# A hybrid decoder layer on one core: another order of the kept weights in memory

## The chip, the cores and the metric

The kernel runs on one core of a Trainium2 chip. The metric is the device time of one execution in microseconds (us), taken as the median of several runs. A core has five engines with a queue of instructions each: TensorE (PE, matrix products; its weight loads are listed as PEld), VectorE (DVE), ScalarE (ACT), GpSimd (POOL) and SyncE (SP), which here only issues transfers. Sixteen DMA engines carry the transfers of the core.

## The reference

One layer over 2048 rows of width 1024, all in float32. A conditioning vector gives shift, scale and gate; the input is normalised, scaled and shifted, and one projection of width 2832 feeds four heads of gated linear attention and eight query heads of attention in a sliding window:

```python
mod = jnp.dot(jax.nn.silu(c), w_ada[l]) + b_ada[l]
shift, scale, gate = jnp.split(mod, 3, axis=-1)
h = rmsnorm(x, g_norm[l]) * (1.0 + scale[:, None, :]) + shift[:, None, :]
proj = jnp.einsum('bsd,de->bse', h, w_in[l])
gq, gk, gv, ga, gz, sq, sk, sv, sz = split_cols(proj, COL_SIZES)
...
y = jnp.einsum('bse,ed->bsd', jnp.concatenate([o_gla, o_swa], axis=-1), w_out[l])
x = x + gate[:, None, :] * y
return rmsnorm(x, g_final)
```

The change concerns only how the parts of `w_in` are kept between their uses.

## The kernel before

**Split weights.** Each float32 weight is split into a high part (rounded to the matrix engine's float32r type) and a low part (the rest). A product is three matmuls: high by high, high by low, low by high. The input weights are therefore read once from the input `in_w_in`, split by ACT (a cast) and POOL or DVE (a subtraction), used, and both parts are stored in a tensor in memory called `wc`, from which later row blocks load them.

**Slots and row blocks.** The 2048 rows go in four blocks of 512 (`u` = 0 to 3). The 2832 columns are nine slots: six "half" slots of 256 columns (qk0, gz0, sz0, qk1, gz1, sz1; two pieces `c` of 128 columns, eight k tiles of 128 rows each) and three wide ones (kv with 272 columns, sq and gv with 512; four pieces `j` of two k tiles). Block 0 starts with qk0, gz0 and sz0 together, with k as the outer loop (`proj_t_outer`, line 943): each k step loads 384 KB of raw weights (`wr_first`), splits them (`part`, line 682) and prepares the normalised input of that k (`hh`, `hl`). After that come sz1/0, gz1/0, kv and so on, one slot after the other; the matmuls of these are called pt (half slots) and pn (wide ones).

**Where the first three slots live.** `first_w` (line 665) puts qk0 into two tiles of 8 KB a partition, `wh_first` and `wl_first`, for the high and the low part; each holds k, column. gz0 and sz0 lie in 16 small tiles of 2 KB a partition, `wh_own` and `wl_own` for each k, each with slot and column. The two first tiles come from the ring of five large weight tiles (`w_tile`, line 414), which the streamed slots use as well: pieces of kv take over the buffers of wh_first, wl_first and then of the sz1/0 tile, and can be filled only when the stores out of these have been done.

**The stores.** `keep_k` (line 693) stores an own tile; two of them (k = 0) go early, those of the last two k after the input's last tile (`keep_parts`, line 701), then the four stores of the first tiles, and the other ten own stores later, behind slot kv (`keep_rest`, line 711).

**Streamed slots.** `slot_w` (line 734) loads the pieces of the other slots. For block 0 it brings raw pieces, splits them into the tile and stores the whole tile; for later blocks it loads the tile from `wc` in two transfers of half the k tiles each (lines 766 and 767).

**What sets the order.** The kernel's own planner (class `Order`) takes each instruction with an estimated duration and writes a fixed order for every engine before anything runs. A DMA counts there by its bytes, an ACT or POOL instruction by a fixed part and its columns. All transfers of the weights go through SP's single queue in that order. A buffer is reused when everything that read it is done.

**Places in memory.** `wc` has one row of 2 × 22656 numbers per partition. A slot's part is ordered piece, part (high or low), k, column.

Of the kernel before, what the change touches and what calls it, by code (L numbers as in the profile page):

```python
# [9 lines left out]
F32 = mybir.dt.float32  # L10
F32R = mybir.dt.float32r
I32 = mybir.dt.int32
AF = mybir.ActivationFunctionType
ALU = mybir.AluOpType
# [4 lines left out]
P = 128  # L19
D = 1024  # L20
S = 2048
KT = D // P
NB = 512
# [19 lines left out]
SLOT_O = {}  # L43
# [7 lines left out]
HB, ZS, VB, GB, QR, WAB, STB, WB = 13, 6, 6, 4, 4, 5, 3, 5  # L51
# [288 lines left out]
def free_size(ap):  # L340
    n = 1
    for d in list(ap.shape)[1:]:
        n *= d
    return n
# [48 lines left out]
def layer_kernel(ctx, tc, x, xT, w_ada, w_gate, b_cols, b_gate, g_cols, c_cols, pos, inv_freq,  # L393
# [3 lines left out]
    V, A, G, SY = [Engine(od, e) for e in ("V", "A", "G", "SP")]  # L397
# [12 lines left out]
    hp = Pool("hp", HB)  # L410
# [3 lines left out]
    def w_tile(name):  # L414
        own = next(w_turn) % WB == WB - 1
        return wp.tile([P, 2 * KT * P], F32R, name=name, tag="w2" if own else "w", bufs=1 if own else WB - 1)
# [7 lines left out]
    def f(ap):  # L424
        return ap.bitcast(F32)


    def mmul(o, l, r, start, stop, bank=None):
        n, m, k = free_size(r), free_size(l), l.shape[0]
        mode = cell = None  # L430
        if l.dtype == F32:
            dur = 2 * max(0.107, n / 1200)
            if k <= 64:
                mode, cell = "rows", l.start_partition()
            elif m <= 64:
                mode, cell = "cols", o.start_partition()
        else:
            dur = max(0.112, n / 2400 + 0.0137)
        return od.add("PE", lambda: T.matmul(o, l, r, start=start, stop=stop), dur,  # L439
                      [l, r] + ([] if start else [o]), [bank if start and bank is not None else o],  # L440
                      mode=mode, cell=cell)
# [82 lines left out]
    near = Pool("near", 1)  # L524
    begin = Pool("begin2", 1, into=ctx2)
# [135 lines left out]
    wc = dram.tile([P, 2 * W_COLS], F32R, name="wc")  # L661
# [3 lines left out]
    def first_w():  # L665


        n = SLOT_N["qk0"]
        t0 = [w_tile(f"w{i}_first").rearrange("p (k n) -> p k n", n=n) for i in "hl"]
        t1 = [[hp.tile([P, 2, n], F32R, name=f"w{'hl'[i]}_own{k}", tag="hh" if i == 0 else "hl")  # L670
               if k < KT - 2 else
               near.tile([P, 2, n], F32R, name=f"w{'hl'[i]}_own{k}", tag=f"qk{i}" if k == KT - 2 else "zs",
                         bufs=2 if k == KT - 2 else ZS)
               for k in range(KT)] for i in range(2)]
        src = w_in[:, 0:3 * KT * n].rearrange("p (k n) -> p k n", n=3 * n)
        raws = {}

        def load(k):
            raws[k] = begin.tile([P, 3, n], F32, name=f"wr_first{k}", tag="st0", bufs=3)
            SY.dma_start(raws[k].rearrange("p a b -> p (a b)"), src[:, k])  # L680

        def part(k):
            raw = raws.pop(k)
            both = ([t[:, k] for t in t0], raw[:, 0]), ([t[k] for t in t1], raw[:, 1:3])
            for d, r in both:
                (G.tensor_copy if k == 0 else A.copy)(d[0], r)
            for d, r in both:
                G.tensor_tensor(d[1], r, f(d[0]), ALU.subtract)
            if k == 0:
                for i in range(2):  # L690
                    keep_k(i, 0)

        def keep_k(i, k, lift=None):
            o = 2 * SLOT_O["gz0"]
            to = wc[:, o:o + 4 * KT * n].rearrange("p (s c i k m) -> p s c i k m", s=2, c=2, i=2, k=KT)
            od.lift = LATER if lift is None else lift
            x = SY.dma_start(f(to[:, :, :, i, k]), f(t1[i][k]).rearrange("p s (c m) -> p s c m", c=2))
            od.lift = 0
            return x

        def keep_parts(after):
            ops = [keep_k(i, k, 0) for k in (KT - 1, KT - 2) for i in range(2)]
            o = 2 * SLOT_O["qk0"]
            to = wc[:, o:o + 2 * KT * n].rearrange("p (c i k m) -> p c i k m", c=2, i=2, k=KT)
            for i in range(2):
                for c in range(2):
                    ops.append(SY.dma_start(f(to[:, c, i]), f(t0[i][:, :, c * P:(c + 1) * P])))
            for x in ops:
                x.deps.add(after)

        def keep_rest():
            after = od.ops[-1]
            for i in range(2):
                for k in range(1, KT - 2):
                    keep_k(i, k, 0).deps.add(after)

        parts = [[[t0[i][:, k] for k in range(KT)] for i in range(2)]]
        for j in range(2):
            parts.append([[t1[i][k][:, j] for k in range(KT)] for i in range(2)])
        return parts, load, part, keep_parts, keep_rest  # L720

    stream, loaded = [], [2, 0]
# [11 lines left out]
    def slot_w(u, name, lift=LIFT):  # L734

        name, _, half = name.partition("/")
        n = SLOT_N[name]
        o = SLOT_O[name]
        wide = name in WIDE
        count = KT // 2 if wide else 2  # L740
        kk, m = (2, n) if wide else (KT, P)
        tiles = {}
        kept = wc[:, 2 * o:2 * (o + KT * n)].rearrange("p (j i k m) -> p j i k m", j=count, i=2, k=kk)
        src = w_in[:, o:o + KT * n].rearrange("p (j k m) -> p j k m", j=count, k=kk)
        step = max(1, NB // m)

        def load(j):
            t = w_tile(f"w_{name}{u}_{j}")[:, :2 * kk * m].rearrange("p (i k m) -> p i k m", i=2, k=kk)
            tiles[j] = t
            od.lift = -lift  # L750
            if u == 0:
                for k in range(0, kk, step):
                    turn = next(raw_turn)
                    if turn < 4 or turn % 7 < 3:
                        raw = stp.tile([P, NB], F32, name=f"wr_{name}{u}_{j}{k}", tag="st")
                    else:
                        raw = keep.tile([P, NB], F32, name=f"wr_{name}{u}_{j}{k}", tag="wst", bufs=4)
                    raw = raw[:, :step * m].rearrange("p (k m) -> p k m", k=step)
                    h_, l_ = [t[:, i, k:k + step] for i in range(2)]
                    SY.dma_start(raw, src[:, j, k:k + step])  # L760
                    A.copy(h_, raw)
                    (G if name in SPLIT_G else V).tensor_tensor(l_, raw, f(h_), ALU.subtract)
                od.lift = STORE
                SY.dma_start(f(kept[:, j]), f(t))
            else:
                for k in range(0, kk, kk // 2):
                    SY.dma_start(f(t[:, :, k:k + kk // 2]), f(kept[:, j, :, k:k + kk // 2]))

        stream.extend([lambda j=j: load(j) for j in ([int(half)] if half else range(count))])

        def w(i, k, c=0):
            return tiles[k // 2][:, i, k % 2] if wide else tiles[c][:, i, k]

        return w

# [7 lines left out]
    hh = [None] * KT  # L783
    hl = [None] * KT
# [58 lines left out]
    def halves(j):  # L843

        return [slice(0, NB // 2), slice(NB // 2, NB)] if j == 0 else [slice(0, NB)]
# [97 lines left out]
    def proj_t_outer(ws, each):  # L943

        ps = []
        for tag in ("mm", "mm", "psc", "psc", "px", "pqk"):
            b = 2 if tag in ("mm", "psc") else 1
            ps.append((mm if tag == "mm" else att).tile([P, NB], F32, name=f"po{len(ps)}", tag=tag, bufs=b))
        for k in range(KT):
            each(k)  # L950
            for h in halves(k):
                for i, w in enumerate(ws):
                    for ct in range(2):
                        cs = slice(ct * P, (ct + 1) * P)
                        p = ps[2 * i + ct]

                        for n, (a, b) in enumerate(((w[0], hh), (w[1], hh), (w[0], hl))):
                            mmul(p[:, h], a[k][:, cs], b[k][:, h], k == 0 and h.start == 0 and n == 0,
                                 k == KT - 1 and n == 2, p)
        return ps  # L960

# [13 lines left out]
    qk = {}  # L975
# [430 lines left out]
    sin = const.tile([P, 16, 32], F32, name="sin")  # L1406
    todo = [(0, n) for n in ORDER0] + [(u, n) for u in range(1, NU) for n in ORDER]
    ws = [slot_w(u, n, LIFT if i > 1 else 0) for i, (u, n) in enumerate(todo)]

    warm(WARM0, None)  # L1410
# [59 lines left out]
    for i, (u, slot) in enumerate(todo):  # L1470
        if u > 0 and slot == ORDER[0]:
            hh, hl = nexth[u]
        w = ws[i]
        name, _, half = slot.partition("/")
# [103 lines left out]
```

## Time and profile before

| what | value |
|---|---|
| median of three runs | 836.94 us (835.5, 836.94, 837.18) |
| the profiled execution | 835.71 us |
| its span, first to last instruction | 834.0 us |
| mean granted TensorE clock | 0.997 of full |
| HBM read, written | 145.26 MB, 54.66 MB |

The page of the profile has the busy time of each engine over the whole span. Other views used below: busy time by stretches, each engine's timeline (start, duration, engine, line, operation, output<-inputs, shape, count, and in brackets the idle time before it with what ended it), the instructions of one tile with their shortest, median and longest duration, and the table of DMA issues (destination<-source, count, size of one, median time to landing). Nearly every instruction is recorded by a helper, so its line is 387 or 439, and instructions are told apart by the names of their tiles.

### The profile page before, as it was taken

What the parts mean: (1) busy time and instruction counts of PE and PEld (TensorE: products, weight loads), DVE (VectorE), ACT (ScalarE), POOL (GpSimd) and SP (SyncE); (2) the same over time, 40 slices, a digit from 0 to 9 for tenths busy, and PEclk for the clock granted to TensorE, in tenths of its full rate; (3) what the DMA queues carried; (4) which work ended last, traced back from release to release, by engine and by line L of the source; (5) the groups of instructions that cost most, each with busy time, mean ns of one, the idle gap of its engine ahead of it and who ended that gap; (6) DMA issues with size and microseconds to landing.
All of it is one profiled execution on the core that took longest, in us unless ns stands there. A gap on an engine that the chain in (4) does not pass through costs nothing.

```text
span 834.0 us, 13255 instructions
## 1 busy us (share of the span) xinstructions
PE 809.6 (97%) x4274; PEld 671.9 (81%) x4274; DVE 597.4 (72%) x1140; ACT 511.0 (61%) x1271; POOL 396.0 (47%) x461
## 2 busy tenths in 40 slices
PE   7998999999999999999999999999999999999995
PEld 6777788879888787888878888888888888888884
DVE  6986567678568978785797747524675766889895
ACT  4567865898556778675587857524677633344431
POOL 4512225456632558645667544322462514665642
PEclk9999999999999999999999999999999999999998
DMA  9969997847448499598887938637467864454432
GB/s 339 377 196 354 388 357 297 288 150 267 174 169 286 142 370 332 180 327 307 284 296 271 380 117 301 219 111 267 143 209 265 288 216 166 141 162 152 140 101 101
DMA packets 118812, 200.81 MB, mean 241 GB/s; under 512 B 10275, under 2 KB 42070, under 8 KB 116054
## 3 DMA queue, kind: packets, MB, share of 16 engines
q1 hardware_dynamic: 117734, 199.91, 68.8%
q8 instruction: 34, 0.56, 0.3%
q14 instruction: 36, 0.29, 0.1%
q10 hardware_dynamic: 1008, 0.05, 0.1%
HBM read 145.26 MB, written 54.66 MB: 240 GB/s over the span
## 4 chain that ended last, share of the span: by engine, by line
PE 67%; DVE 3%; ACT 2%; DMA 2%; POOL 2%; issue 1%; DVEq 0%; ACTq 0%; POOLq 0%
PE pt L439 18%; PE pn L439 17%; PE ya L439 10%; PE ys L439 9%; PE ppo L439 3%; PE psc L439 2%; PE po L439 2%; DMA xt<-in_xT 1%; PE ppt L444 1%; PE pc L439 1%; DMA xn<-in_x 1%; PE pms L439 1%; PE pu L439 1%; ACT s L387 1%; DVE hl L387 1%
## 5 line engine op out<-in xcount | busy, mean ns | idle before, releaser
L439 PE MATMUL pn<-w_gv,hh 128*128 128x512 f32 x256 | 85.6, 398 | 0.0
L439 PE MATMUL pn<-w_sq,hh 128*128 128x512 f32 x256 | 82.0, 395 | 0.0
L439 PE MATMUL pt<-hh,w_gz 128*128 128x512 f32 x224 | 74.8, 397 | 0.1
L439 PE MATMUL pt<-hh,w_qk 128*128 128x512 f32 x224 | 74.9, 399 | 0.0
L439 PE MATMUL pt<-hh,w_sz 128*128 128x512 f32 x224 | 72.8, 394 | 0.2 <-ACT hh L387 0.2
L387 POOL TENSOR_TENSOR y<-u,y 128x512 f32<-128x512 f32 x28 | 42.4, 1518 | 56.7 <-DVE y L387 33.3
L387 ACT ACTIVATE ge<-ge 128x512 f32<-128x512 f32 x96 | 60.6, 631 | 11.3 <-DVE ge L387 10.0
L387 ACT ACTIVATE s<-s,nm 128x129 f32<-128x129 f32 x128 | 51.4, 402 | 19.5 <-DVE nm L387 18.9
L387 POOL TENSOR_TENSOR xt<-xt,rstd 128x512 f32<-128x512 f32 x27 | 38.5, 1433 | 41.1 <-DMA xt<-in_xT 25.6
L439 PE MATMUL pn<-w_kv,hh 128*128 128x272 f32 x256 | 51.1, 292 | 5.1 <-ACT zs L387 1.8
L439 PEld LDWEIGHTS pn<-w_sq,hh 128*128 128x128 f32 x256 | 47.5, 188 | 10.5 <-issue 0.5
L439 PEld LDWEIGHTS pn<-w_gv,hh 128*128 128x128 f32 x256 | 47.1, 188 | 8.6
L439 PE MATMUL ys<-woht,m 128*128 128x512 f32 x168 | 53.4, 392 | 0.0
L439 PE MATMUL pn<-w_gv,hl 128*128 128x512 f32 x128 | 50.4, 394 | 0.0
L439 PE MATMUL pn<-w_sq,hl 128*128 128x512 f32 x128 | 50.3, 393 | 0.0
L387 POOL TENSOR_TENSOR s<-s,den 128x512 f32<-128x512 f32 x32 | 35.2, 1103 | 30.8 <-DVE den L387 24.1
L439 PE MATMUL ya<-wohb,m 128*128 128x512 f32 x152 | 49.6, 392 | 0.0
L439 PEld LDWEIGHTS pt<-hh,w_sz 128*128 128x128 f32 x224 | 41.9, 188 | 9.1 <-ACT hh L387 0.5
L387 POOL TENSOR_TENSOR o<-o,zs 128x128 f32<-128x128 f32 x64 | 34.4, 558 | 31.0 <-DVE o L387 25.5
L439 PEld LDWEIGHTS pt<-hh,w_gz 128*128 128x128 f32 x224 | 41.6, 188 | 9.0 <-DVE w_gz L387 0.6
L387 ACT CAST m<-mr 128x512 fp32r<-128x512 f32 x39 | 23.1, 618 | 41.9 <-PE ya L439 20.7
L439 PEld LDWEIGHTS pt<-hh,w_qk 128*128 128x128 f32 x224 | 41.6, 188 | 7.9
(272 smaller groups left out, 2388.2 us busy)
## 6 DMA issues: line engine op xcount, KB each, us to landing
w_sz<-wc SPq DMA_DIRECT2D x24, 512.0 KB, 6.4
w_sq<-wc SPq DMA_DIRECT2D x24, 512.0 KB, 7.6
w_qk<-wc SPq DMA_DIRECT2D x24, 512.0 KB, 7.0
w_gv<-wc SPq DMA_DIRECT2D x24, 512.0 KB, 8.6
w_gz<-wc SPq DMA_DIRECT2D x24, 512.0 KB, 6.5
mr<-mixd SPq DMA_DIRECT2D x32, 256.0 KB, 3.0
y<-in_x SPq DMA_DIRECT2D x32, 256.0 KB, 3.4
out<-y SPq DMA_DIRECT2D x32, 256.0 KB, 2.2
```

The source lines that it names most:

```text
L387: return order.add(eng, lambda: real(*args, **kw), dur, ins, outs, lock=lock, nbytes=nbytes)
L439: return od.add("PE", lambda: T.matmul(o, l, r, start=start, stop=stop), dur, [l, r] + ([] if start else [o]), [bank if start and bank is ...
L444: return od.add("PE", lambda: T.transpose(o, i, ident), 0.109, [i, ident], [o], mode="few" if o.shape[0] <= 32 else None)
```

## The change

The part of a slot in `wc` is ordered piece, k, part, column in place of piece, part, k, column, and the streamed tiles in the core have the same order (part inside k). The two first tiles hold four k tiles each in place of one part each, ordered column piece, k, part, column. The own tiles hold one slot each (both parts of it) in place of one part of two slots. `part` splits into three equal tiles of 256 columns a k step, so three casts and three subtractions, in place of two of each. The number and size of the stores stay.

```diff
-        t0 = [w_tile(f"w{i}_first").rearrange("p (k n) -> p k n", n=n) for i in "hl"]
-        t1 = [[hp.tile([P, 2, n], F32R, name=f"w{'hl'[i]}_own{k}", tag="hh" if i == 0 else "hl")
...
+        half = KT // 2
+        t0 = [w_tile(f"w_first{i}").rearrange("p (c k i m) -> p c k i m", c=2, k=half, i=2) for i in range(2)]
+
+        def own(k, j):
+            name = f"w_own{k}{j}"
+            if k < KT - 2:
+                t = hp.tile([P, NB], F32R, name=name, tag="hh" if j == 0 else "hl")
+            elif k == KT - 2:
+                t = near.tile([P, NB], F32R, name=name, tag=f"qk{j}", bufs=2)
+            else:
+                t = near.tile([P, NB], F32R, name=name, tag="zs", bufs=ZS)
+            return t.rearrange("p (c i m) -> p c i m", c=2, i=2)
+
+        t1 = [[own(k, j) for j in range(2)] for k in range(KT)]
...
         def part(k):
             raw = raws.pop(k)
-            both = ([t[:, k] for t in t0], raw[:, 0]), ([t[k] for t in t1], raw[:, 1:3])
-            for d, r in both:
-                (G.tensor_copy if k == 0 else A.copy)(d[0], r)
-            for d, r in both:
-                G.tensor_tensor(d[1], r, f(d[0]), ALU.subtract)
+            homes = [t0[k // half][:, :, k % half]] + t1[k]
+            for j, t in enumerate(homes):
+                (G.tensor_copy if k == 0 else A.copy)(t[:, :, 0], raw[:, j])
+            for j, t in enumerate(homes):
+                G.tensor_tensor(t[:, :, 1], raw[:, j], f(t[:, :, 0]), ALU.subtract)
...
+        def kept(j):
+            o = 2 * SLOT_O[("qk0", "gz0", "sz0")[j]]
+            return wc[:, o:o + 2 * KT * n].rearrange("p (c k i m) -> p c k i m", c=2, k=KT, i=2)
+
+        def keep_k(j, k, lift=None):
             od.lift = LATER if lift is None else lift
-            x = SY.dma_start(f(to[:, :, :, i, k]), f(t1[i][k]).rearrange("p s (c m) -> p s c m", c=2))
+            x = SY.dma_start(f(kept(j + 1)[:, :, k]), f(t1[k][j]))
...
         def keep_parts(after):
-            ops = [keep_k(i, k, 0) for k in (KT - 1, KT - 2) for i in range(2)]
-            o = 2 * SLOT_O["qk0"]
-            to = wc[:, o:o + 2 * KT * n].rearrange("p (c i k m) -> p c i k m", c=2, i=2, k=KT)
+            ops = [keep_k(j, k, 0) for k in (KT - 1, KT - 2) for j in range(2)]
             for i in range(2):
                 for c in range(2):
-                    ops.append(SY.dma_start(f(to[:, c, i]), f(t0[i][:, :, c * P:(c + 1) * P])))
+                    ops.append(SY.dma_start(f(kept(0)[:, c, i * half:(i + 1) * half]), f(t0[i][:, c])))
...
-        kept = wc[:, 2 * o:2 * (o + KT * n)].rearrange("p (j i k m) -> p j i k m", j=count, i=2, k=kk)
+        kept = wc[:, 2 * o:2 * (o + KT * n)].rearrange("p (j k i m) -> p j k i m", j=count, i=2, k=kk)
...
-            t = w_tile(f"w_{name}{u}_{j}")[:, :2 * kk * m].rearrange("p (i k m) -> p i k m", i=2, k=kk)
+            t = w_tile(f"w_{name}{u}_{j}")[:, :2 * kk * m].rearrange("p (k i m) -> p k i m", i=2, k=kk)
...
-                    h_, l_ = [t[:, i, k:k + step] for i in range(2)]
+                    h_, l_ = [t[:, k:k + step, i] for i in range(2)]
...
-                    SY.dma_start(f(t[:, :, k:k + kk // 2]), f(kept[:, j, :, k:k + kk // 2]))
+                    SY.dma_start(f(t[:, k:k + kk // 2]), f(kept[:, j, k:k + kk // 2]))
...
-            return tiles[k // 2][:, i, k % 2] if wide else tiles[c][:, i, k]
+            return tiles[k // 2][:, k % 2, i] if wide else tiles[c][:, k, i]
```

The remaining lines of the diff rename the loops over these tiles.

More of the change, by code (lines that the diff above doesn't have):

```diff
@@ L668, in first_w @@
         n = SLOT_N["qk0"]
-        t0 = [w_tile(f"w{i}_first").rearrange("p (k n) -> p k n", n=n) for i in "hl"]
-        t1 = [[hp.tile([P, 2, n], F32R, name=f"w{'hl'[i]}_own{k}", tag="hh" if i == 0 else "hl")
[L671 to L674, printed above, removed]
+        half = KT // 2
[10 more added lines that the diff above has]
+        t1 = [[own(k, j) for j in range(2)] for k in range(KT)]
         src = w_in[:, 0:3 * KT * n].rearrange("p (k n) -> p k n", n=3 * n)
@@ L678, in load @@
         def load(k):
-            raws[k] = begin.tile([P, 3, n], F32, name=f"wr_first{k}", tag="st0", bufs=3)
-            SY.dma_start(raws[k].rearrange("p a b -> p (a b)"), src[:, k])
+            raws[k] = begin.tile([P, 3, 2, P], F32, name=f"wr_first{k}", tag="st0", bufs=3)
+            SY.dma_start(raws[k].rearrange("p a b c -> p (a b c)"), src[:, k])
         def part(k):
             raw = raws.pop(k)
-            both = ([t[:, k] for t in t0], raw[:, 0]), ([t[k] for t in t1], raw[:, 1:3])
-            for d, r in both:
-                (G.tensor_copy if k == 0 else A.copy)(d[0], r)
-            for d, r in both:
-                G.tensor_tensor(d[1], r, f(d[0]), ALU.subtract)
-            if k == 0:
[L690 to L695, printed above, removed]
+            homes = [t0[k // half][:, :, k % half]] + t1[k]
[3 more added lines that the diff above has]
+                G.tensor_tensor(t[:, :, 1], raw[:, j], f(t[:, :, 0]), ALU.subtract)
+            if k == 0:
+                for j in range(2):
+                    keep_k(j, 0)
+        def kept(j):
+            o = 2 * SLOT_O[("qk0", "gz0", "sz0")[j]]
+            return wc[:, o:o + 2 * KT * n].rearrange("p (c k i m) -> p c k i m", c=2, k=KT, i=2)
+        def keep_k(j, k, lift=None):
             od.lift = LATER if lift is None else lift
-            x = SY.dma_start(f(to[:, :, :, i, k]), f(t1[i][k]).rearrange("p s (c m) -> p s c m", c=2))
+            x = SY.dma_start(f(kept(j + 1)[:, :, k]), f(t1[k][j]))
             od.lift = 0
@@ L712, in keep_rest @@
             after = od.ops[-1]
-            for i in range(2):
+            for j in range(2):
                 for k in range(1, KT - 2):
-                    keep_k(i, k, 0).deps.add(after)
-        parts = [[[t0[i][:, k] for k in range(KT)] for i in range(2)]]
+                    keep_k(j, k, 0).deps.add(after)
+        parts = [[[[t0[k // half][:, c, k % half, i] for c in range(2)] for k in range(KT)] for i in range(2)]]
         for j in range(2):
-            parts.append([[t1[i][k][:, j] for k in range(KT)] for i in range(2)])
+            parts.append([[[t1[k][j][:, c, i] for c in range(2)] for k in range(KT)] for i in range(2)])
         return parts, load, part, keep_parts, keep_rest
@@ L953, in proj_t_outer @@
                     for ct in range(2):
-                        cs = slice(ct * P, (ct + 1) * P)
                         p = ps[2 * i + ct]
                         for n, (a, b) in enumerate(((w[0], hh), (w[1], hh), (w[0], hl))):
-                            mmul(p[:, h], a[k][:, cs], b[k][:, h], k == 0 and h.start == 0 and n == 0,
+                            mmul(p[:, h], a[k][ct], b[k][:, h], k == 0 and h.start == 0 and n == 0,
                                  k == KT - 1 and n == 2, p)
```

## The prediction

> **What bounds the kernel now.** I read the page first, then the busy time by stretches, then each engine's timeline where a stretch shows TensorE idle.
>
> ```profile
> span 834.0 us, 13255 instructions
> ...
> PE 809.6 (97%) x4274; PEld 671.9 (81%) x4274; DVE 597.4 (72%) x1140; ACT 511.0 (61%) x1271; POOL 396.0 (47%) x461
> ...
> DMA packets 118812, 200.81 MB, mean 241 GB/s; under 512 B 10275, under 2 KB 42070, under 8 KB 116054
> ```
>
> TensorE (PE) is idle for 834.0 − 809.6 = 24.4 us, and the change leaves its matmuls alone. Only those idle stretches can move, so the question is which of them hang on the kept weights' transfers. The columns below are the stretch and its length, then busy us (and instructions) of PE, weight loads, DVE, ACT and POOL, then clock, DMA share and GB/s:
>
> ```profile
> 20.00:40.00 20.00, 17.74 (x82) 14.35 (x81) 19.54 (x26) 10.81 (x24) 12.57 (x12) 1.00 0.99 383
> 40.00:60.00 20.00, 20.00 (x89) 16.45 (x88) 18.72 (x34) 13.85 (x29) 4.63 (x8) 1.00 0.65 190
> 60.00:80.00 20.00, 15.21 (x92) 12.46 (x91) 12.24 (x30) 13.96 (x26) 2.79 (x6) 1.00 1.03 367
> 80.00:100.00 20.00, 20.00 (x105) 16.92 (x104) 13.71 (x31) 16.52 (x35) 8.15 (x15) 1.00 0.99 368
> ```
>
> The stretch 60 to 80 is the one to see: PE loses 4.8 us there while the DMA engines are full. From 40 to 60 and from 80 to 100 PE has no gap. Its timeline puts a releaser on each longer gap:
>
> ```profile
> 62.70 0.52 PE L439 MATMUL pn<-w_kv,hh 128*128 128x272 f32 x2 [1.16 <-ACT zs L387]
> 65.40 0.87 PE L439 MATMUL pn<-w_kv,hh 128*128 128x272 f32 x2 [0.93 <-ACT w_kv L387]
> 70.31 0.52 PE L439 MATMUL pn<-w_kv,hh 128*128 128x272 f32 x2 [0.68 <-ACT zs L387]
> 72.21 0.40 PE L439 MATMUL pn<-w_kv,hh 128*128 128x272 f32 x1 [0.62 <-ACT w_kv L387]
> 76.90 0.52 PE L439 MATMUL pn<-w_kv,hh 128*128 128x272 f32 x2 [1.19 <-ACT kvr L387]
> ```
>
> Together 4.58 us, each put down to ACT. ACT's own rows show what stands behind it:
>
> ```profile
> 58.26 1.30 ACT L387 ACTIVATE ge<-ge 128x512 f32<-128x512 f32 x2 [2.67 <-DVE ge L387]
> 61.43 0.74 ACT L387 CAST w_kv<-wr_kv 128x272 fp32r<-128x272 f32 x2 [1.88 <-DMA wc<-wh_first]
> 62.07 0.58 ACT L387 COPY zs<-pt 128x512 f32<-128x512 f32 x1
> ...
> 64.93 0.42 ACT L387 CAST w_kv<-wr_kv 128x272 fp32r<-128x272 f32 x1 [1.74 <-DMA wc<-wl_first]
> ...
> 68.73 0.74 ACT L387 CAST w_kv<-wr_kv 128x272 fp32r<-128x272 f32 x2 [0.70 <-DMA wc<-w_sz]
> 69.67 0.59 ACT L387 COPY zs<-pt 128x512 f32<-128x512 f32 x1 [0.20 <-PE pt L439]
> ...
> 71.74 0.42 ACT L387 CAST w_kv<-wr_kv 128x272 fp32r<-128x272 f32 x1 [0.58 <-DMA wr_kv<-in_w_in]
> ...
> 76.47 0.39 ACT L387 COPY kvr<-pn 128x272 f32<-128x272 f32 x1
> ```
>
> The casts that fill the kv tiles wait for the stores that free their buffers: the tiles of the first slot (wh_first, wl_first), then w_sz. ACT runs in its written order, so the copy that empties PE's bank (zs) stands behind a cast that waits for a store, and PE behind that copy. SP issues these stores in one queue with the raw loads:
>
> ```profile
> 54.18 0.50 SPq L387 DMA_DIRECT2D wc<-wh_first  x1
> ...
> 57.38 3.08 SPq L387 DMA_DIRECT2D wc<-wl_first  x2
> ...
> 61.83 1.20 SPq L387 DMA_DIRECT2D wc<-w_sz  x1
> ```
>
> So this stage is bound by what the DMA engines carry between about 50 and 72 us, and the two kinds of store that the change reshapes lie ahead of every gate in it.
>
> **The change part by part: the stores.** Sizes per issue and count, from the table of issues:
>
> ```profile
> wc<-wh_own SPq DMA_DIRECT2D x8, 256.0 KB, 6.0
> wc<-wl_own SPq DMA_DIRECT2D x8, 256.0 KB, 4.3
> wc<-wh_first SPq DMA_DIRECT2D x2, 512.0 KB, 4.7
> wc<-wl_first SPq DMA_DIRECT2D x2, 512.0 KB
> ```
>
> By the access patterns of the code, all of these now move in pieces of 512 B: the own tiles because their place in memory has runs of 128 columns, the first tiles because the tile in the core has them. After, own tiles have runs of 1 KB and first tiles of 4 KB on both sides. In the batch ahead of the gates lie four own stores (1.05 MB) and the four first stores (2.10 MB). What 512 B pieces cost is read from the rates:
>
> ```profile
> 50.00:62.00 12.00, 11.54 (x51) 9.21 (x50) 10.06 (x21) 7.37 (x15) 0.00 (x0) 1.00 1.04 304
> 104.00:112.00 8.00, 8.00 (x37) 6.63 (x36) 5.35 (x10) 6.39 (x13) 1.30 (x1) 1.00 1.12 331
> 118.00:132.00 14.00, 14.00 (x101) 11.58 (x100) 7.45 (x18) 6.79 (x15) 5.75 (x12) 1.00 1.02 422
> ```
>
> The first row is this batch, the second the later own stores, the third a full stretch whose stores (w_sq, w_qk) and loads have long runs. All three have the DMA share at about 1, so the difference lies in what a full engine carries. From 331 a 512 B piece takes 16 × 512 / 331 = 24.7 ns on one of 16 engines, and from 422 a 2 KB piece 77.7 ns; the line through both gives 42 ns at 1 KB, which is 386 GB/s, and for 4 KB I take no more than the measured 422. Then the own stores go from 3.17 to 2.72 us and the first from 6.34 to 4.97: **1.8 us** less. The first row gives the other end: 3.65 MB in 12 us, of which 0.50 MB are loads at some 400, leaves 3.15 MB of stores at 293 GB/s. The same steps give 3.58 to 2.86 and 7.16 to 4.97: **2.9 us**. I take 2.3, between two ends that are near each other.
>
> The Trainium skill speaks against this: its page "DMA: Bandwidth & Descriptors", section Specifications, gives 512 B as the least transfer for line rate. By that rule the edit saves nothing here; the rates above differ by a fifth, so this trace does not bear it out, though its windows mix loads and stores. The same page of the Trainium skill, section "Why small descriptors are slow (HBM only)", has a fixed cost of about 3 cycles beside 16 beats for 512 B; an estimate from that page is 8% on the own and 14% on the first stores, 1.1 us in all, and by it the sum below would be 835.8.
>
> **What that is worth.** Follow the gates. The wh_first gate has the four own and half of the first stores ahead of it, so it comes 1.1 to 1.8 us earlier. ACT was free from 59.56, so its cast starts at 60.3 to 59.6 instead of 61.43, the bank is emptied at 60.9 to 61.5, and PE, done with w_gz at 61.54, meets at most a tenth: 1.1 of the 1.16 goes. The wl_first gate comes 1.8 to 2.9 earlier, so the second gap goes too (0.93; a rest of some 0.3 at the low end). Everything queued behind, the w_sz store and the last raw kv tile, moves by the same 1.8 to 2.9; the gap of 0.62 goes at the high end. What is late next: the 0.68 and the 1.19 are ACT emptying a bank that PE has only just filled, or ACT's unbroken run from 71.74 to 76.86 (no row in between carries a wait), and they travel along. So at most 1.16 + 0.93 + 0.62 = 2.7 us can go, at least the 1.8 by which the last gate moves: I take **2.2 us**.
>
> **The start.** Each of the eight k steps splits three equal tiles in place of one and a double one:
>
> ```profile
> L387 POOL TENSOR_TENSOR wl_first<-wr_first,wh_first x8: 739/748/1212, 14.8 to 44.5; 128x256 fp32r<-128x256 f32 x8
> L387 ACT CAST wh_first<-wr_first x7: 388/392/399, 18.4 to 44.1; 128x256 fp32r<-128x256 f32 x7
> ...
> L387 POOL TENSOR_TENSOR wl_own<-wr_first,wh_own x8: 1274/1316/1625, 15.5 to 46.2; 128x512 fp32r<-128x512 f32 x8
> ...
> L387 ACT CAST wh_own<-wr_first x7: 606/616/624, 18.7 to 45.5; 128x512 fp32r<-128x512 f32 x7
> ```
>
> POOL: 3 × 0.748 − (0.748 + 1.316) = 0.18 us per step, 1.4 in eight. ACT: 3 × 0.392 − 1.008 = 0.17, 1.2 in seven. Neither engine is full there (POOL 12.57, ACT 10.81 of 20 us), but DVE is (19.54), and the trace shows it held up beside POOL:
>
> ```profile
> 25.27 1.32 POOL L387 TENSOR_TENSOR wl_own<-wr_first,wh_own 128x512 fp32r<-128x512 f32 x1
> 25.64 1.49 DVE L387 SCALAR_TENSOR_TENSOR hl<-xt,ashift,hh 128x512 fp32r<-128x512 f32 x1
> 47.47 0.81 DVE L387 SCALAR_TENSOR_TENSOR hl<-xt,ashift,hh 128x512 fp32r<-128x512 f32 x1 [0.91 <-issue]
> 49.59 0.39 PE L439 MATMUL po<-hl,wh_first 128*128 128x512 f32 x1
> ```
>
> The same instruction takes 0.81 us alone and 1.49 beside the long POOL instruction. Shorter POOL pieces hold it for less (0.75 at most in place of 1.32), while one more of them can meet it. DVE's last tile is done at 48.28 and PE first needs it at 49.59: 1.3 us of cover. I put the start at 0, between −0.7 (two such hold-ups halved) and the price of the third rival. If the cover went, the stores, which wait for that last tile, would go late with it. The order of all instructions is computed from estimated durations, so 15 changed steps may also shuffle ACT's order; I value that at 0, and it is the fourth rival.
>
> **The later loads.** Tiles for the later row blocks come in runs of 4 KB in place of 2 KB:
>
> ```profile
> w_sz<-wc SPq DMA_DIRECT2D x24, 512.0 KB, 6.4
> ...
> 355.73 0.52 PE L439 MATMUL pn<-w_kv,hh 128*128 128x272 f32 x2 [0.44 <-DMA w_kv<-wc]
> ```
>
> They are issued far ahead, and PE names such a load as its releaser once, for 0.44 us. I count 0, at best −0.4. The casts and subtractions of the streamed tiles write with a stride now, in the same number of elements and instructions; PE still reads 128 or 512 adjacent columns. The later own stores lie where PE has no gap. All this counts 0.
>
> **Sum.** 835.7 (the profiled execution; its span is 834.0, with 1.7 around it) − 2.2 = 833.5. The median shown, 836.94, is 1.2 above the profiled one, so the forecast is 836.94 − 2.2 = **834.7**, with 834.0 to 835.2 for its own ends.
>
> **Rivals.**
> (1) *Pieces of 512 B cost nothing extra.* The batch was slow for another reason: stores, not short runs. For it: no row here times a lone store. Against it: the 422 row holds stores too. All gates stay: 836.9.
> (2) *A larger gain.* The gates move, ACT's new order parts the bank copies from the casts, and all 4.58 us of the five gaps go: 832.4. Against it: 1.87 of them follow PE and ACT themselves.
> (3) *Slower: the start.* Each of the eight added POOL instructions holds one more DVE instruction for 1.49 − 0.81 = 0.68 us: 5.4 us on DVE's chain, less 1.3 of cover, is 4.1, less the gain 2.2 is +1.9: 838.8. It loses from six such meetings on (6 × 0.68 = 4.1 against 1.3 + 2.2 = 3.5). Against it: the pieces are shorter.
> (4) *Shuffled order.* One more bank copy falls behind a waiting cast, twice the size of the first gap (2 × 1.16): the gain is spent, 837.0.
>
> **How the numbers follow.** Forecast 0.47; no extra cost of short runs 0.17; larger gain 0.13; slower start 0.13; shuffled order 0.10. A change of 0.2% (1.7 us) is about what a measurement of this kernel can tell from none. Faster by more: most of the forecast (0.39; its low end is 1.8) and the larger gain, 0.52. Within: the rest of the forecast, rival 1 and half of rival 4, 0.30. Slower: rival 3 and the rest of 4, 0.18. The range runs from 832.2 (the larger gain with some of the loads' 0.4) to 838.0 (rival 4 and half of rival 3), leaving about 0.15 to 0.2 out.
>
> **What would show it.** Packets fall by 26,000 to some 92,700 if every run is one packet (4096 + 512 for the 12,288 of the first slots, half of the 36,864 of the later loads), those under 2 KB to some 27,700. In 50 to 62 us the rate passes 350 GB/s, and the cast behind wh_first starts before 60.4. PE's gaps of 1.16 and 0.93 are gone, those before zs at 70 and kvr at 77 stay. Wrong would be: the same rate with fewer packets (rival 1); hl of the last k later than 49.6 (rival 3); a new ACT wait ahead of a bank copy (rival 4).

## The result and the profile after

The changed kernel takes **831.88 us** (median of four runs, 830.73 to 832.8) against 837.06 for the kernel before on the same chip (835.5 to 837.7): a ratio of 0.9944, with a 95% interval of 0.9929 to 0.9959. The forecast was 834.7 in a range of 832.2 to 838.0. The sign was right, the size was not: the gain is 5.2 us against 2.2 forecast. As it stands, 831.88 lies 0.3 us below the range; on the median from which the forecast was reckoned (836.94) the ratio gives 832.25, at its lower edge. On a second chip, where it ran again beside the experiments, the ratio was 0.9961 (0.9948 to 0.9975), a gain of 3.0 us, so some 3 to 5 us are to be explained.

The page of the changed kernel has the span, the engines' busy time and the packets:

```profile
span 830.3 us, 13284 instructions
...
PE 810.8 (98%) x4274; PEld 674.6 (81%) x4274; DVE 593.5 (71%) x1140; ACT 509.2 (61%) x1278; POOL 391.4 (47%) x470
...
DMA packets 92700, 200.81 MB, mean 242 GB/s; under 512 B 10275, under 2 KB 27734, under 8 KB 89942
```

The packets are those forecast (92,700, and 27,700 under 2 KB), so the runs became as long as the diff says. TensorE's idle time fell from 24.4 to 830.3 − 810.8 = 19.5 us, 4.9 less; its busy time rose by 1.2 us, though it has the same 4274 matmuls. Both need a reason. Some 0.9 us of the 4.9 lie in the first 20 us and may be this execution's own: PE is idle there for 3.61 us before and 2.75 after, but for 3.78 in the changed kernel's profile from the second chip. The busy time by stretches of the changed kernel (columns as in the prediction):

```profile
20.00:40.00 20.00, 18.78 (x88) 15.54 (x88) 19.77 (x30) 13.00 (x33) 16.01 (x19) 1.00 1.02 402
...
50.00:62.00 12.00, 12.00 (x55) 9.94 (x54) 11.15 (x23) 8.91 (x19) 0.00 (x0) 1.00 1.01 334
...
60.00:80.00 20.00, 18.45 (x123) 16.82 (x122) 16.52 (x40) 17.77 (x37) 4.66 (x9) 1.00 1.01 369
...
392.00:400.00 8.00, 5.29 (x18) 3.96 (x17) 7.90 (x10) 3.53 (x6) 5.29 (x5) 0.82 0.27 98
```

From 60 to 80 PE loses 1.55 us in place of 4.79: the stage that the prediction looked at gave 3.2. From 20 to 40 it loses 1.22 in place of 2.26. But from 392 to 400 it loses 2.7 us and the granted clock is 0.82, where the kernel before lost nothing:

```profile
392.00:400.00 8.00, 8.00 (x39) 6.55 (x38) 6.88 (x9) 4.79 (x10) 5.50 (x6) 1.00 0.40 138
```

PE's timeline of the changed kernel has the gaps:

```profile
64.72 0.39 PE L439 MATMUL pn<-w_kv,hh 128*128 128x272 f32 x1 [0.23 <-ACT w_kv L387]
...
65.52 0.52 PE L439 MATMUL pn<-w_kv,hh 128*128 128x272 f32 x2 [0.41 <-ACT zs L387]
...
74.08 0.52 PE L439 MATMUL pn<-w_kv,hh 128*128 128x272 f32 x2 [0.92 <-ACT kvr L387]
...
397.43 0.80 PE L439 MATMUL pr<-dgh,ones_r 128*128 128x512 f32 x1 [2.71 <-DVE dgh L387]
...
400.58 0.40 PE L439 MATMUL pr<-dgl,ones_r 128*128 128x512 f32 x1
```

The five gaps of the start are three small ones. The wait of 2.71 us at 397 is new and has nothing to do with memory: it comes from the planner. With three equal tiles a k step in place of two, its estimates differ from the first step on, and it wrote another order for the whole kernel. The store of w_sz, for one, is issued at 46.6 us in place of 61.83. So three things changed at once: **the length of the runs, the three-way split, and the order of everything.** The experiments take them apart.

### The profile page after: what moved, and what is told of

Read it like the earlier page. It is cut to its first block, busy times and chain, and to the rows that moved or that the text cites. A ratio compares the mean times of both kernels' runs of the same rounds, so it can differ in the third digit from the quotient of the medians.

```text
span 830.3 us, 13284 instructions
## 1 busy us (share of the span) xinstructions
PE 810.8 (98%) x4274; PEld 674.6 (81%) x4274; DVE 593.5 (71%) x1140; ACT 509.2 (61%) x1278; POOL 391.4 (47%) x470
## 2 busy tenths in 40 slices
DMA packets 92700, 200.81 MB, mean 242 GB/s; under 512 B 10275, under 2 KB 27734, under 8 KB 89942
## 4 chain that ended last, share of the span: by engine, by line
PE 81%; DVE 5%; ACT 3%; DMA 3%; issue 1%; SPq 1%; POOL 0%; DVEq 0%; ACTq 0%
PE pn L439 25%; PE pt L439 22%; PE ya L439 10%; PE ys L439 9%; PE psc L439 3%; PE ppo L439 3%; PE po L439 3%; PE ppt L444 1%; PE pc L439 1%; DMA xn<-in_x 1%; PE pu L439 1%; DMA xt<-in_xT 1%; PE pq L444 1%; PE pms L439 1%; DMA wc<-w_gz 1%
## 5 line engine op out<-in xcount | busy, mean ns | idle before, releaser
L439 PE MATMUL pt<-hh,w_sz 128*128 128x512 f32 x224 | 74.5, 395 | 0.0
L387 POOL TENSOR_TENSOR xt<-xt,rstd 128x512 f32<-128x512 f32 x27 | 36.8, 1366 | 34.5 <-DMA xt<-in_xT 31.0
L387 POOL TENSOR_TENSOR o<-o,zs 128x128 f32<-128x128 f32 x64 | 32.3, 523 | 36.8 <-DVE o L387 35.2
```

What stands on the lines that cost most here:

```text
L387: return order.add(eng, lambda: real(*args, **kw), dur, ins, outs, lock=lock, nbytes=nbytes)
```

## The experiments

Each ratio is to the kernel before, timed together with it on the same chip. "Stores" are those of the first three slots. Where the later loads are of 2 KB, those of kv are of 1 KB, and those of qk0 (in e3 and g1 also gz0 and sz0) stay at 4 KB.

| kernel | order | split | stores | later loads | chip | median us | ratio (95%) |
|---|---|---|---|---|---|---|---|
| e2b | old | 3 | 512 B | 2 KB | A | 834.87 | 0.9993 (0.9983 to 1.0002) |
| e2 | old | 3 | 1 and 4 KB | 4 KB | A | 832.57 | 0.9967 (0.9954 to 0.9980) |
| e1 | new | 3 | 512 B | 2 KB | A | 836.61 | 1.0012 (0.9999 to 1.0025) |
| e3 | new | 3 | 1 and 4 KB | 2 KB | A | 833.61 | 0.9977 (0.9965 to 0.9988) |
| changed kernel again | new | 3 | 1 and 4 KB | 4 KB | B | 833.32 | 0.9961 (0.9948 to 0.9975) |
| e2 again | old | 3 | 1 and 4 KB | 4 KB | B | 832.33 | 0.9954 (0.9942 to 0.9966) |
| g1 | old | 3 | 1 and 4 KB | 2 KB | B | 832.32 | 0.9952 (0.9940 to 0.9964) |
| f1 | new, gate products held | 3 | 1 and 4 KB | 4 KB | B | 831.85 | 0.9946 (0.9934 to 0.9957) |
| f2 | new, dg kept together | 3 | 1 and 4 KB | 4 KB | C | 830.21 | 0.9931 (0.9914 to 0.9948) |
| f3 | new, dg together in all blocks | 3 | 1 and 4 KB | 4 KB | C | 831.85 | 0.9947 (0.9929 to 0.9966) |
| s1 | old | 6 pieces on POOL | 1 and 4 KB | 4 KB | C | 831.34 | 0.9943 (0.9928 to 0.9958) |

The kernel before had medians of 835.79 (A), 836.33 (B) and 836.1 (C).

### The old order with long runs (e2), and without (e2b)

The planner is told the old durations for the split's instructions and takes the second and third as one group, so that it writes the order of the kernel before, with the added instructions standing beside their neighbours:

```diff
+            cast = (0.2 + 512 / 1300, 0.041) if k == 0 else (0.2 + 512 / 1200, 0.094)
+            def both(make, told):
+                make(0)
+                with od.together():
+                    for j in (1, 2):
+                        od.told = told[j - 1]
+                        make(j)
+                        od.told = None
```

e2b has besides this the short runs, in the tiles of the core and in memory (and for the later loads, by the lines shown with e3 below):

```diff
-        t0 = [w_tile(f"w_first{i}").rearrange("p (c k i m) -> p c k i m", c=2, k=half, i=2) for i in range(2)]
+        t0 = [w_tile(f"w_first{i}").rearrange("p (k i c m) -> p c k i m", c=2, k=half, i=2) for i in range(2)]
...
-            return wc[:, o:o + 2 * KT * n].rearrange("p (c k i m) -> p c k i m", c=2, k=KT, i=2)
+            return wc[:, o:o + 2 * KT * n].rearrange("p (c k i m) -> p c k i m" if j == 0 else "p (c i k m) -> p c k i m", c=2, k=KT, i=2)
```

> Every engine has the order of the kernel before (the three-way split is entered in the planner with the old durations), but all runs are long as in the changed kernel. If the long runs bring the gain, 2.2 us by the forecast: 834 to 835, with the gaps of 1.16 and 0.93 us gone. If only the new order does: 836 to 837 with those gaps in place.

> The order of the kernel before and its short runs; only the split in three equal tiles is new. If the split brings something at the start, TensorE's k = 1 starts near 23.3 us in place of 24.25 and the time is near 836. If not: 837.0, start at 24.2 or later. By the rival of a slower start: above 837.5.

On chip A the split alone went from 835.79 to 834.87, 0.9 us, with an interval that reaches no change; the long runs on top of it went from 834.87 to 832.57, 2.3 us, with intervals of the ratios that do not overlap. The batch of stores shows in the stretch from 50 to 62 us, first of e2b, then of e2:

```profile
50.00:62.00 12.00, 11.77 (x54) 9.48 (x52) 10.18 (x21) 8.24 (x17) 0.00 (x0) 1.00 1.05 308
```

```profile
50.00:62.00 12.00, 12.00 (x59) 10.13 (x58) 10.85 (x23) 8.28 (x17) 0.00 (x0) 1.00 1.03 363
```

With the DMA engines full in both, 308 GB/s become 363: the last column is the prediction's "350 or more". The two stretches do not hold quite the same transfers, since in e2 the batch ends sooner and loads follow it. The batch can be timed from end to end too. It begins with the first transfer that SP issues after the last hl, and ends with the second of the casts that wait for the first tiles' stores. SP's timeline of the kernel before has its beginning (its end, 64.93, stands in the prediction):

```profile
48.35 1.78 SPq L387 DMA_DIRECT2D wr_kv<-in_w_in  x4
```

SP's and ACT's timelines of e2b (a helper's line is 392 in this kernel):

```profile
47.33 1.77 SPq L392 DMA_DIRECT2D wr_kv<-in_w_in  x4
```

```profile
60.36 0.74 ACT L392 CAST w_kv<-wr_kv 128x272 fp32r<-128x272 f32 x2 [1.44 <-DMA wc<-w_first]
...
63.64 0.42 ACT L392 CAST w_kv<-wr_kv 128x272 fp32r<-128x272 f32 x1 [1.53 <-DMA wc<-w_first]
```

and of e2:

```profile
46.81 1.77 SPq L392 DMA_DIRECT2D wr_kv<-in_w_in  x4
```

```profile
59.06 0.74 ACT L392 CAST w_kv<-wr_kv 128x272 fp32r<-128x272 f32 x2 [0.63 <-DMA wc<-w_first]
...
61.48 0.42 ACT L392 CAST w_kv<-wr_kv 128x272 fp32r<-128x272 f32 x1 [0.66 <-DMA wc<-w_first]
```

The batch lasts 64.93 − 48.35 = 16.6 us before, 16.3 in e2b and 14.7 in e2. **Long runs shorten it by 1.6 us against e2b (1.9 against before, which has another split)**; the instructions of every engine stand in the same order in e2b and e2. But it also begins earlier: 48.35, 47.33, 46.81. The first of these two steps belongs to the split, and the rows of one tile, hl, say why. The columns are count, shortest, median and longest duration in ns, first and last start. Of the kernel before:

```profile
L387 DVE SCALAR_TENSOR_TENSOR wa<-wa,pb x12: 1206/1208/1212, 23.4 to 43.9; 128x1024 f32<-128x1024 f32 x12
...
L387 DVE SCALAR_TENSOR_TENSOR hl<-xt,ashift,hh x4: 742/1146/1493, 25.6 to 47.5; 128x512 fp32r<-128x512 f32 x4
```

Of e2b:

```profile
L392 DVE SCALAR_TENSOR_TENSOR hl<-xt,ashift,hh x4: 799/922/947, 25.8 to 46.3; 128x512 fp32r<-128x512 f32 x4
```

The longest hl falls from 1.49 to 0.95 us. The first hl of e2b stands beside a POOL subtraction like this:

```profile
25.43 0.75 POOL L392 TENSOR_TENSOR w_own<-wr_first,w_own 128x256 fp32r<-128x256 f32 x1
25.81 0.92 DVE L392 SCALAR_TENSOR_TENSOR hl<-xt,ashift,hh 128x512 fp32r<-128x512 f32 x1
```

In the prediction's rows of the kernel before, the subtraction ends at 25.27 + 1.32 = 26.59, 0.95 us after hl has started, and hl takes 1.49. Here it ends at 26.18, 0.37 after hl's start, and hl takes 0.92. Both leave 0.54 to 0.55 us: hl waits to the end of the POOL instruction that it meets, and a piece of 0.75 us ends sooner than one of 1.32. From the first of these four hl to the start of the last, 21.8 us become 20.5. But for 0.9 us before the last hl, in both kernels, DVE is nearly full there, so its chain is 1.3 us shorter, and the stores, which wait for its last tile, begin about 1.0 earlier. On PE nothing was gained: k = 1 starts at 24.41 us, where the expectation of e2b asked for 23.3. The second step, from 47.33 to 46.81, is the two runs' own start: the first hl of this form stands at 25.81 in e2b and at 25.30 in e2. The wa rows are the control: their second input lies in PSUM, and all twelve take the same 1.21 us beside the same POOL instructions. The Trainium skill, page "SBUF — State Buffer", section "Who interferes with whom", says so: a DVE instruction with two inputs in SBUF contends with a GpSimd instruction that reads SBUF; one with at most one such input, outside the 2-port performance modes, does not. This trace agrees, with 1.49 us at most against 0.74 at least for hl, and 1.21 for every wa.

PE's gaps show how the split and the long runs share the gain. Its timelines of e2b and of e2:

```profile
61.64 0.52 PE L444 MATMUL pn<-w_kv,hh 128*128 128x272 f32 x2 [0.23 <-ACT zs L392]
64.11 0.87 PE L444 MATMUL pn<-w_kv,hh 128*128 128x272 f32 x2 [0.71 <-ACT w_kv L392]
69.03 0.52 PE L444 MATMUL pn<-w_kv,hh 128*128 128x272 f32 x2 [0.68 <-ACT zs L392]
71.13 0.39 PE L444 MATMUL pn<-w_kv,hh 128*128 128x272 f32 x1 [0.83 <-ACT w_kv L392]
75.83 0.52 PE L444 MATMUL pn<-w_kv,hh 128*128 128x272 f32 x2 [1.20 <-ACT kvr L392]
```

```profile
63.88 0.73 PE L444 MATMUL pt<-hh,w_gz 128*128 128x512 f32 x2 [0.21 <-DVE w_gz L392]
...
67.10 0.52 PE L444 MATMUL pn<-w_kv,hh 128*128 128x272 f32 x2 [0.68 <-ACT zs L392]
...
73.23 0.52 PE L444 MATMUL pn<-w_kv,hh 128*128 128x272 f32 x2 [1.20 <-ACT kvr L392]
```

In e2 the gaps of 1.16, 0.93 and 0.62 are gone, 0.68 and 1.20 travelled along, and 0.21 is new, as forecast for the long runs. But 0.93 of the 1.16 had gone in e2b, with the split and short runs, because the batch began 1.0 us earlier there. From e2b to e2 the gaps of 0.23, 0.71 and 0.83 go and 0.21 comes: 1.6 us in this stage. Where the other 0.7 of the 2.3 us in time came from, the runs do not show. In e2's repeat a gap of 0.33 is left in place of the 0.62.

### The new order with short runs (e1)

The changed kernel with the short runs of e2b, in the planner's new order.

```diff
-        t0 = [w_tile(f"w_first{i}").rearrange("p (c k i m) -> p c k i m", c=2, k=half, i=2) for i in range(2)]
+        t0 = [w_tile(f"w_first{i}").rearrange("p (k i c m) -> p c k i m", c=2, k=half, i=2) for i in range(2)]
```

> Every engine has the order of the changed kernel and the split in three, but the stores of the first slots go in pieces of 512 B again and the later loads (but those of qk0) in runs of 2 KB. If the long runs bring the gain (my forecast: 2.2 us of it), the casts of the kv tiles wait for stores again and the time is 834 to 835. If the new order brings it, the time stays within 1 us of 831.9 and TensorE's idle time from 60 to 80 us stays below 2.5 us.

836.61, a little slower than the kernel before, and 1.6 to 2.6 us above the 834 to 835 that were expected if the long runs bring the gain. So the new order by itself is no gain. PE's timeline of e1:

```profile
67.97 0.39 PE L439 MATMUL pn<-w_kv,hh 128*128 128x272 f32 x1 [3.19 <-ACT w_kv L387]
...
401.83 0.50 PE L439 MATMUL pr<-dgh,ones_r 128*128 128x512 f32 x1 [2.71 <-DVE dgh L387]
```

With long runs the first of these waits is the 0.23 us at 64.72 above. In e1's chain of work that ended last, the last store of the first tiles stands before it, from 61.93 to 65.57 us, and then 1.93 us that the profile puts down to nothing; in the changed kernel that store is issued at 59.69. The second wait is the changed kernel's own, so the long runs have no part in it. In this order they are worth 836.61 − 833.61 = 3.0 us (e3, same chip) in place of 2.3. Part of that is the clock, which is at 0.59 and 0.55 in the two stretches of 2 us from 68 to 72 us of e1, behind the wait of 3.19.

### The later loads (e3, g1)

Both put the streamed slots back to part, k in memory and in the tile, so that their later loads have runs of 2 KB (kv 1 KB); the first three slots keep the new places. e3 is in the new order, g1 in the old.

```diff
+        new = name in ('qk0', 'gz0', 'sz0')
+        pat = "(k i m) -> p k i m" if new else "(i k m) -> p i k m"
...
-                SY.dma_start(f(kept[:, j]), f(t))
+                SY.dma_start(f(kept[:, j].rearrange("p " + pat, i=2, k=kk)), f(t))
```

> The changed kernel, with its order and its long stores of the first slots, but all other slots are kept and loaded in the old layout (loads in runs of 2 KB in place of 4, kv 1 KB in place of 2). I counted the later loads at 0 to 0.4 us: 831.9 to 832.3. If the later loads carry part of the gain: 833 or more.

> Old order, stores of the first slots in long runs, all other slots kept and loaded in the old layout (2 KB, kv 1 KB). If the stores carry the gain: as e2_again within 0.7 us, with the gaps of 1.16 and 0.93 us gone. If the later loads do: 1.5 us or more slower than e2_again.

g1 is 0.9952 beside 0.9954 for e2 on chip B: loads of 4 KB are worth nothing that these runs can tell. e3 (0.9977, chip A) lies above the changed kernel's 0.9944 and 0.9961 on other chips, and alone would have hinted at a loss; but e2 too stands 0.0013 higher on chip A than on chip B, and with that shift the changed kernel would be at 0.9974 on A.

### The changed kernel and e2 on one chip

> The changed kernel itself, timed on one chip with the three that follow, so that they can be compared with it. Ratio to before near 0.994 as at first.

> Old order, all runs long, once more beside the changed kernel. If the new order is worth nothing on balance (it gains 1 to 2 us in the first 80 us and gives 2.7 back at 397 us), it lies within 1 us of the changed kernel. If the order carries what my forecast missed: slower than it by 2 us or more.

0.9961 and 0.9954, with intervals that overlap: the new order gains nothing over the old with long runs. It gives with one hand (60 to 80 us, for one: PE busy 18.45 in the changed kernel, and in e2 on chip A)

```profile
60.00:80.00 20.00, 17.62 (x117) 15.52 (x116) 15.57 (x36) 16.19 (x33) 5.91 (x11) 1.00 0.98 368
```

and takes with the other, at 397 us. DVE's and then POOL's timeline of the changed kernel there:

```profile
393.53 2.65 DVE L387 SCALAR_TENSOR_TENSOR dgl<-ident,rr,dgh 128x128 fp32r<-128x128 f32 x2
396.10 1.28 DVE L387 TENSOR_SCALAR dgh<-ident,rr 128x128 fp32r<-128x128 f32 x1
...
398.73 0.35 DVE L387 SCALAR_TENSOR_TENSOR dgl<-ident,rr,dgh 128x128 fp32r<-128x128 f32 x1
```

```profile
393.02 3.01 POOL L387 TENSOR_TENSOR qk<-qk,zs 128x512 f32<-128x512 f32 x2
395.99 1.30 POOL L387 TENSOR_TENSOR wor<-wor,wor 128x512 f32<-128x512 f32 x1
```

Eight small products on DVE (dgh, dgl) make the scale of the last row block. Alone dgl takes 0.35 us and dgh 0.28; beside a POOL product of 1.3 to 1.5 each takes about as long as that product. The three in the first two rows take 3.85 us, from 393.53 to 397.38, where 0.35 + 0.35 + 0.28 = 1.0 would do, by the times alone: a difference of 2.9, more than the whole wait of 2.71. dgh reads only one tile (ident) and a column of scalars and is held as well. In the planner's order PE's pr stands in the middle of the matmuls of w_sq, so all of PE waited for them.

### Holding the gate products (f1)

The first theory: the two gate products on POOL (`qk<-qk,zs`) are the ones that hold DVE, so they are made to wait for the last dgl.

```diff
+        if u == 3:
+            for h in range(2):
+                held[HOLD + (h,)].deps.add(d)
```

> The changed kernel, with the two gate products of POOL that lie beside VectorE's small dgh and dgl instructions at 393 to 397 us ordered behind them. If VectorE is held up by POOL there, the wait of 2.71 us before pr shrinks below 1 us and the time falls by about 2 us, to a ratio near 0.992. If something else is late there, the wait stays and the time is that of the changed kernel.

A miss. The ratio is 0.9946, and the wait is still 2.69 us. POOL's timeline of f1:

```profile
392.89 3.01 POOL L388 TENSOR_TENSOR wor<-wor,wor 128x512 f32<-128x512 f32 x2
395.87 1.30 POOL L388 TENSOR_TENSOR qk<-qk,zs 128x512 f32<-128x512 f32 x1
```

The planner only put other products in the freed place, and they hold DVE just as long: both dgl together take 2.64 us.

### Keeping the small products together (f2, f3)

f2 makes the eight products one group of the planner in the last row block, f3 in every block.

```diff
+        with od.together() if u == 3 else ExitStack():
+            for t in range(TPU):
                 V.tensor_scalar(dg[0][:, t], ident, rr[:, t:t + 1], None, op0=ALU.mult)
```

> The changed kernel, with VectorE's eight dgh and dgl instructions of the last row block kept together in VectorE's order, so that no other instruction of its own comes between them. If the wait of 2.7 us before pr, and the lower clock behind it, are due to these being strung out beside POOL's products, the wait goes and the time falls by 2.5 to 4 us against the changed kernel: ratio to before 0.991 to 0.993. If not: 0.995 to 0.996 as the changed kernel.

> The same for all three later row blocks; the order changes from about 124 us on. Under the first theory a ratio of 0.991 to 0.993 again; a new wait elsewhere would take part of it back.

f2 takes 830.21 us and has the lowest ratio of the study, 0.9931 (0.9914 to 0.9948). DVE's timeline of f2, and its busy time:

```profile
386.88 0.28 DVE L387 TENSOR_SCALAR dgh<-ident,rr 128x128 fp32r<-128x128 f32 x1
...
388.95 0.35 DVE L387 SCALAR_TENSOR_TENSOR dgl<-ident,rr,dgh 128x128 fp32r<-128x128 f32 x1
```

```profile
392.00:400.00 8.00, 8.00 (x39) 6.63 (x38) 5.09 (x10) 6.39 (x11) 8.00 (x9) 1.00 0.66 191
```

All eight are done in 2.4 us with POOL idle, the wait is gone, and PE is busy for 8.00 of 8 us at full clock, beside 5.29 at 0.82 in the changed kernel. f2 moves the eight together and to a place where POOL is idle, so it does not part the two. f3 lost the wait at 397 as well, but its planner wrote still another order; its PE timeline has a wait in a new place:

```profile
284.18 0.72 PE L439 MATMUL psc<-kst,qs 128*128 128x256 f32 x4 [1.93 <-DVE s L387]
```

Against the changed kernel f2 was not timed on one chip, and their intervals overlap; that it is faster than that kernel rests on the trace.

### Smaller pieces on POOL (s1)

e2 with POOL's subtractions cut once more, to 128 columns.

```diff
+                    for i, (j, c) in enumerate((j, c) for j in js for c in range(2)):
+                        od.told = 0.041 if i else 0.2 + n / 470
+                        G.tensor_tensor(homes[j][:, c, 1], raw[:, j, c], f(homes[j][:, c, 0]), ALU.subtract)
```

> Old order, long runs, POOL's subtractions of the first slots cut once more, into pieces of 128 columns. If shorter POOL pieces hold VectorE up for less, VectorE's last hl (46.7 us in e2, 48.3 in the kernel before) comes at 46.7 or earlier although POOL issues 24 more instructions, and the time is that of e2 or a little less (ratio 0.994 to 0.996). If the gain at the start has another source, POOL's extra 0.1 to 0.2 us an instruction shows: the last hl at 47.5 or later, ratio 0.997.

0.9943 (0.9928 to 0.9958), beside 0.9954 and 0.9967 for e2 on other chips. The direction agrees, but the intervals overlap. From the first of the four hl to the start of the last it is 20.3 us, beside 20.5 in e2: halving the pieces a second time brought 0.2 us of the chain where the first brought 1.3, and SP's first transfer of the batch comes at 46.88, no earlier than e2's 46.81.

## Why the prediction was right, and where it was not

**The stores: right.** The batch was expected 1.8 to 2.9 us shorter and is 1.6 with the same split, just under the low end. The Trainium skill's rule, weighed in the prediction (page "DMA: Bandwidth & Descriptors", section Specifications: 512 B suffice for line rate), does not hold for these stores: the stretch that carries them moves 308 GB/s with runs of 512 B and 363 with longer ones, at a DMA share of 1.05 and 1.03. Rival 1 falls with e2b and e2, which differ in the runs alone: 834.87 against 832.57.

**What it is worth: right in size, and by the way foretold in part.** 2.2 us were taken and 2.3 measured between e2b and e2. The gaps of 1.16, 0.93 and 0.62 went and 0.68 and 1.19 stayed, in the old order in which the prediction reasoned. But the prediction let the long runs take the first gap, and 0.93 of its 1.16 went with the split alone; the gaps give the long runs 1.6 us. That 2.2 and 2.3 agree so closely is in part luck. The lower of the forecast's own ends, 834.0, takes the batch's 2.9 us, where the gaps allow 2.7 at most, 834.2. Rival 2, all five gaps, falls as a mechanism: waits for zs and kvr stay in the changed kernel too (0.41 and 0.92). Its 832.4 us still come closer to 831.88 than the forecast does.

**The start: the term that was mis-sized.** It stood at 0, with −0.7 as its best end. The mechanism was named, but one step was wrong: the cover of 1.3 us was read from PE alone, which needs the last hl late. The prediction itself says that the stores wait for that tile, and drew this only for the bad case. They begin when DVE is done, so the 1.3 us that DVE's chain lost pulled the whole batch forward by 1.0. Nor were there only two such hold-ups: three hl rows fell, from 1.49, 1.48 and 1.53 to 0.92, 0.92 and 0.81, and some of that went into short waits for other engines. The 0.81 us that the prediction took for hl alone holds some waiting itself: that hl starts at 47.47, inside a POOL subtraction that runs from 46.22 to 47.72. In time the split is worth 0.9 us on chip A, with an interval that includes 0; that it gains rests on the shorter chain and on PE's first gap. Rival 3, a slower start, had the sign reversed. Split and long runs together are e2 against the kernel before: 3.2 us on chip A and 4.0 on chip B, inside the second interval of the changed kernel (2.1 to 4.3 us), at the low end of the first (3.4 to 5.9).

**The later loads: right.** Counted 0, and the ratios of e2 and g1 agree within 0.0002, with intervals of 0.0012 on each side.

**The shuffled order: valued at 0, and 0 on balance, but by two effects that cancel.** Rival 4 expected one new wait of some 2.3 us at a bank copy. The new wait came (2.71 us), in another place and by another mechanism, and the new order's better start paid for it: e2 and the changed kernel differ by 0.0007 in the ratio, within the intervals, and on chip A e3 lies 1.0 us above e2, with intervals that overlap. With short runs the order's price shows (e1 against e2b, 1.0012 against 0.9993). That the first measurement of the changed kernel lies 0.0017 below the second is within the intervals; the runs do not say whether chips differ in this.

## What to carry to other kernels

When an instruction gets shorter, ask who else waits for it: cover on the busiest engine says nothing of the stores that the same tile releases. Where a planner writes the order, an edit's own effect and the new order's are two changes; pin the order to see the first, then look for the one long wait that the second brought. A small DVE instruction such as dgl or dgh is best placed where POOL is idle, as in f2. A long POOL instruction beside a full DVE is worth cutting once, as e2b's chain shows; a second cut brought little in s1.

## What the runs showed of the hardware

A wait of 2.7 us on PE costs more than itself here. The stretches of the changed kernel around 397 us:

```profile
396.00:398.00 2.00, 0.57 (x1) 0.50 (x2) 1.97 (x3) 0.00 (x0) 1.29 (x2) 0.80 0.28 91
398.00:400.00 2.00, 2.00 (x6) 1.59 (x5) 1.93 (x4) 1.24 (x2) 0.00 (x0) 0.50 0.00 0
400.00:402.00 2.00, 2.00 (x9) 1.55 (x9) 0.47 (x2) 0.95 (x2) 1.78 (x3) 0.85 0.01 3
```

The granted clock is 0.80, 0.50 and 0.85 there, and pr<-dgh takes 0.80 us where pr<-dgl, 3 us later, takes 0.40. That is about (1 − 0.50) × 2 + (1 − 0.85) × 2 = 1.3 us on top of the 2.7, about as much as PE's 1.2 us of additional busy time. In f3 a wait of 1.93 us was followed by a stretch of 2 us at 0.50 as well:

```profile
286.00:288.00 2.00, 2.00 (x6) 1.52 (x6) 1.89 (x6) 0.87 (x3) 0.88 (x1) 0.50 0.00 0
```

The same followed the wait of 3.19 us in e1. The longest wait between matmuls that left the clock at 1.00 in these traces is one of 1.49 us, in the kernel before at 24.25 us; where between 1.49 and 1.93 us the clock begins to fall, and whether the length of the wait alone decides it, no run shows.

DVE and POOL hold each other both ways. In the kernel before, the hl that starts at 40.94 us, ahead of the POOL subtraction that starts at 41.22, takes 0.74 us, and the subtraction 1.62 in place of 1.31.
